# Sums of squares of the attention's heads: accumulated by ScalarE head by head, in place of one square and a reduction by VectorE

## The chip, the cores and the metric

The kernel runs on one core of one Trainium2 chip. The metric is the device time of one execution in microseconds (us), lower is better. The engines of a core are PE (TensorE, matmuls), DVE (VectorE), ACT (ScalarE), POOL (GpSimd) and SP (SyncE, here only a queue that issues transfers). Each takes its own instructions in the order in which the program lists them, and waits for the others by semaphores.

## The reference

Two layers of a trunk run over 640 tokens: 128 context tokens and 512 latent tokens that share the weights. In each layer the normed input goes through one projection `w_in`, and its columns feed three parallel mixers: a short gated convolution, windowed attention with 8 query heads and 2 key heads of 64, and a bidirectional gated DeltaNet. Their outputs go through `w_out`, and a SwiGLU channel mixer follows. What the change touches is the norm of queries and keys, per token and head:

```
def _rms(x, g):
    xf = x.astype(F32)
    y = xf * lax.rsqrt(jnp.mean(xf * xf, axis=-1, keepdims=True) + EPS)
    return (y * g.astype(F32)).astype(x.dtype)

q = _rms(q.reshape(bsz, n, N_Q_HEADS, HEAD_DIM), p['q_norm_g'])
k = _rms(k.reshape(bsz, n, N_KV_HEADS, HEAD_DIM), p['k_norm_g'])
```

For each token the squares of the 64 values of a head are summed: 8 sums for queries and 2 for keys.

## The kernel before, in words

Products are made in three passes of a high and a low part. A weight block of 128x1024 lands in `raw`, ACT rounds it to `whi` and DVE subtracts to get `wlo` (helper `split`, L172 and L173); PE multiplies high by high, high by low and low by high. L199, L201 and L202 are these three for products whose output has channels in its partitions (320 tokens at a time), and L627, L628 and L629 for products that have 128 tokens in their partitions.

The mixer of a layer is made of steps that a string of letters (`SEQ`) lists, among them `q` (queries of four heads, twice a layer), `k` (keys), `J` and `i` (inversion of triangular blocks for the DeltaNet), `h` and `g` (norm of DeltaNet queries `qd` and their products) and `s` (one step of the DeltaNet scan). The letters set the order in which the steps are written; the framework's scheduler then merges the instructions of neighbouring steps on each engine, by its own estimate of when each could run, so a step that gets other instructions can change the order of all those around it.

In the step `q`, PE makes for each of the 5 token tiles a product `pmm` of 128x256 (four heads), ACT copies it to `qv` (L1171), `headss` takes the squares (`asq`, L1077, ACT) and sums them per head into `qss` (L1078, DVE), and ACT's queue sends `qv` to memory (L1173). After the second `q` the inverse roots of all 40 sums are taken by DVE (`rsqrt_dve`, L219 to L234). The step `k` does the same with two heads a tile (`kraw`, `kss`). So `headss` runs 15 times in a layer: 10 times with four heads and 5 times with two.

What lies around the first `q`, in this order on DVE: the end of an inversion (L1010, L1012), its transposes (L1019 to L1022), the copies that PE's next products read (`adx`, L1029) and that make the inverse (`MK`, L1047), two `wlo` for the next weight blocks, then the sums of the DeltaNet queries (`dss`, L816, from the squares `dsq` that ACT makes at L814), their roots, the second inversion (L886 to L912) and the scaling of `qd` (L819). `scp` (L1148) is ACT's copy of a product of the short convolution, `scy` its convolution (L613 to L615), and `Ld` (L886) the blocks that the second inversion starts from.

Of the kernel before, what the change touches and what calls it, by code (L numbers as in the profile page):

```python
# [12 lines left out]
AF = mybir.ActivationFunctionType  # L13
ALU = mybir.AluOpType
AX = mybir.AxisListType
# [93 lines left out]
def hybrid_trunk_kernel(  # L109
# [8 lines left out]
    V, A, G, PE = nc.vector, nc.scalar, nc.gpsimd, nc.tensor  # L118
# [471 lines left out]
    def mixer(l, mp, hs, early_half, fill, first, later):  # L590
# [10 lines left out]
        def sm(tag, name, n, bufs):  # L601
            return mp.tile([128, n], F32, tag=tag, name=name, bufs=bufs)
# [471 lines left out]

        def headss(src, dst, nh):
            sq = sm("asq", "asq", 256, 2)
            A.activation(sq[:, 0:nh * 64], src, AF.Square)  # L1077
            V.tensor_reduce(out=dst, in_=sq[:, 0:nh * 64].rearrange("p (h d) -> p h d", d=64), axis=AX.X, op=ALU.add)  # L1078

        gcs = []  # L1080
        def tables():
# [83 lines left out]
        def queries(hb):  # L1165
            wq = [load_w(wslice(win, kk, 4, 768 + hb * 256, 256), 4, 256) for kk in (0, 4)]
            for t in range(NT):
                pt = pmm()
                tm_product(pt[:, 0:256], wq, t)
                qv = sm("qv", "qv", 256, 2)  # L1170
                A.copy(qv, pt[:, 0:256])  # L1171
                headss(qv, qss[:, t, hb * 4:hb * 4 + 4], 4)
                nc.scalar.dma_start(out=qscr[t, :, hb * 256:(hb + 1) * 256], in_=qv)  # L1173
            if hb == 1:
                rsqrt_dve(qss.rearrange("p t h -> p (t h)"), NT * 8, 1.0 / 64, EPS, ((rq.rearrange("p t h -> p (t h)"), lambda y: y, 0.125),), "q")


        def keys():
# [8 lines left out]
            for t in range(NT):  # L1187
                pt = pmm()
                tm_product(pt[:, 0:256], wkv, t)
                A.copy(kraw[:, t], pt[:, 0:128])  # L1190
                if t == 0:
                    nv = sm("qv", "nv", 256, 2)
                    A.copy(nv[:, 0:128], pt[:, 128:256])
                    nc.scalar.dma_start(out=new_v[0, l].rearrange("s v d -> s (v d)"), in_=nv[:, 0:128])
                put_values(pt[:, 128:256], t)
                headss(kraw[:, t], kss[:, t], 2)
# [355 lines left out]
    with tc.tile_pool(name="f0", bufs=1, reuse_waits="tile") as fp:  # L1552
# [14 lines left out]
        for t in range(NT):  # L1567
            sq = wp.tile([128, DM], F32, tag="raw", name="sqx", bufs=RAW_BUFS)
# [333 lines left out]
```

## Time and profile before

| | us |
|---|---|
| median of 3 runs | 1764.85 |
| lowest and highest of them | 1759.53, 1777.67 |
| the profiled execution, its own time | 1756.52 |
| its span, first to last instruction | 1754.6 |

Busy time of the profiled execution: PE 1663.1 us (95% of the span), DVE 1239.5 (71%), ACT 781.9 (45%), POOL 138.6 (8%). PE is the engine that is nearly always busy. A row of the timeline gives the start in us from the span's start, the duration, the engine, the line, the operation, the tiles and in brackets the time that the engine was idle before it and what it then waited for. Instructions of one engine that do not depend on each other overlap a little, so what an instruction takes from its queue is read from start to start.

### The profile page before, as it was taken

The numbers are of one execution on the slowest core, as the hardware profiler recorded it, in microseconds if no ns is written. First come the engines' busy times: TensorE is split into PE (matmuls) and PEld (weight loads), VectorE is DVE, ScalarE is ACT, GpSimd is POOL, SyncE is SP. The second block draws the span as 40 slices with busy tenths as digits, with TensorE's granted clock in tenths as the row PEclk, the third lists the DMA queues.
The fourth block names the chain that finished last, engine by engine and source line by source line (L and its number), as shares of the span: only waits on it lengthen the run. The fifth ranks groups of instructions, "written<-read, shape, count | busy, mean of one in ns | idle before, by whom it ended". The sixth has DMA issues, their size and how long they took to land. (4 is left out here: it accounts for less than half of the span.)

```text
span 1754.6 us, 34156 instructions
## 1 busy us (share of the span) xinstructions
PE 1663.1 (95%) x13677; PEld 1486.4 (85%) x13677; DVE 1239.5 (71%) x2780; ACT 781.9 (45%) x1620; POOL 138.6 (8%) x254
## 2 busy tenths in 40 slices
PE   6998999999999999999999889999998999999998
PEld 4887875488899999999988879655898999999998
DVE  4899667766856767667677994876578667667664
ACT  4555344645543433434465542555365343434342
POOL 1111112002000000000022001120030000000000
PEclk8998999999999999999999989999999999999999
DMA  9412233655534223222232221445722222222212
GB/s 341 130 49 71 87 98 130 210 162 162 156 117 127 85 70 88 77 87 66 73 116 61 64 72 58 151 151 160 239 72 83 87 74 73 85 84 76 81 61 61
DMA packets 207693, 188.42 MB, mean 107 GB/s; under 512 B 12782, under 2 KB 182702, under 8 KB 207534
## 3 DMA queue, kind: packets, MB, share of 16 engines
q1 hardware_dynamic: 192519, 170.97, 31.3%
q10 hardware_dynamic: 15015, 15.26, 2.7%
q8 instruction: 108, 1.77, 0.4%
q14 instruction: 51, 0.42, 0.1%
HBM read 168.64 MB, written 17.56 MB: 106 GB/s over the span
## 5 line engine op out<-in xcount | busy, mean ns | idle before, releaser
L172 ACT CAST whi<-raw 128x1024 fp32r<-128x1024 f32 (+1 forms) x102 | 100.0, 981 | 166.9 <-PE pmx L201 74.7
L173 DVE TENSOR_TENSOR wlo<-raw,whi 128x1024 fp32r<-128x1024 f32 (+1 forms) x102 | 115.8, 1138 | 24.5 <-ACT whi L172 24.2
L202 PE MATMUL pmm<-hh,wlo 128*128 128x320 f32 x336 | 108.0, 323 | 6.4 <-DVE wlo L173 6.3
L199 PE MATMUL pmm<-hh,whi 128*128 128x320 f32 x336 | 109.0, 326 | 4.5 <-ACT dnp L656 3.2
L582 DVE SCALAR_TENSOR_TENSOR xt<-pmx,mod,xt 128x128 f32<-128x128 f32 (+2 forms) x168 | 69.1, 434 | 50.4 <-PE pmx L202 48.5
L201 PE MATMUL pmm<-hl,whi 128*128 128x320 f32 x320 | 103.0, 322 | 0.0
L199 PE MATMUL pmm<-acth,whi 128*128 128x320 f32 x320 | 99.8, 312 | 1.7 <-DVE xt L582 1.7
L199 PE MATMUL pmx<-acth,whi 128*128 128x320 f32 x320 | 99.2, 310 | 0.1
L202 PE MATMUL pmm<-acth,wlo 128*128 128x320 f32 x320 | 99.2, 310 | 0.0
L201 PE MATMUL pmx<-actl,whi 128*128 128x320 f32 x320 | 99.0, 309 | 0.0
L201 PE MATMUL pmm<-actl,whi 128*128 128x320 f32 x320 | 98.9, 309 | 0.0
L202 PE MATMUL pmx<-acth,wlo 128*128 128x320 f32 x320 | 98.9, 309 | 0.0
L582 DVE SCALAR_TENSOR_TENSOR xt<-pmm,mod,xt 128x128 f32<-128x128 f32 (+2 forms) x168 | 68.6, 434 | 33.2 <-PE pmm L202 22.1
L172 ACT CAST whi<-rawd 128x1024 fp32r<-128x1024 f32 x40 | 42.0, 1050 | 102.8 <-PE pmx L201 93.9
L383 POOL TENSOR_TENSOR acc<-acc,sq 128x320 f32<-128x320 f32 x24 | 25.8, 1074 | 619.6 <-ACT sq L382 619.2
L202 PEld LDWEIGHTS pmm<-hh,wlo 128*128 128x128 f32 x336 | 65.3, 195 | 8.0 <-DVE wlo L173 7.2
L199 PEld LDWEIGHTS pmm<-hh,whi 128*128 128x128 f32 x336 | 65.6, 195 | 6.5 <-ACT dnp L656 4.0
L628 PE MATMUL pmm<-wlo,hh 128*128 128x256 f32 x240 | 69.8, 291 | 0.7 <-DVE wlo L173 0.6
L627 PE MATMUL pmm<-whi,hh 128*128 128x256 f32 x240 | 70.0, 293 | 0.0
L629 PE MATMUL pmm<-whi,hl 128*128 128x256 f32 x240 | 69.6, 290 | 0.0
L299 PE MATMUL pdn<-adaw,c 128*32 128x256 f32 x640 | 63.3, 399 | 5.4 <-DMA adaw<-in_ada_w_dram 5.4
L173 DVE TENSOR_TENSOR xlo<-rawo,xhi 128x1024 fp32r<-128x1024 f32 x40 | 49.0, 1224 | 27.2 <-ACT xhi L172 26.4
(560 smaller groups left out, 5587.2 us busy)
## 6 DMA issues: line engine op xcount, KB each, us to landing
adaw<-in_ada_w_dram SPq DMA_DIRECT2D x80, 512.0 KB, 4.1
raw<-in_w_down_dram SPq DMA_DIRECT2D x44, 512.0 KB, 3.4
raw<-in_w_in_dram SPq DMA_DIRECT2D x36, 512.0 KB, 3.8
rawo<-in_w_gate_dram SPq DMA_DIRECT2D x40, 256.0 KB, 3.6
rawd<-in_w_gate_dram SPq DMA_DIRECT2D x40, 256.0 KB, 3.4
rawd<-in_w_up_dram SPq DMA_DIRECT2D x40, 256.0 KB, 3.4
rawo<-in_w_up_dram SPq DMA_DIRECT2D x40, 256.0 KB, 3.2
araw<-in_ada_w_dram SPq DMA_DIRECT2D x16, 512.0 KB, 11.4
```

Source lines behind the costliest of these rows:

```text
L172: (hi_eng or A.copy)(hi, src)
L173: (lo_eng or V).tensor_tensor(out=lo, in0=src, in1=hi.bitcast(F32), op=ALU.subtract)
L199: mm(o, lhsT=wh[:, k], rhs=ah, start=k == 0, stop=False)
L201: mm(o, lhsT=wh[:, k], rhs=al, start=False, stop=False)
L202: mm(o, lhsT=wl[:, k], rhs=ah, start=False, stop=not lead and k == n - 1)
L299: mm(pr[32 * q:32 * q + 32, 0:256], lhsT=c32[:, k], rhs=raw[:, q * 256:(q + 1) * 256], start=k == 0, stop=k == 7)
L383: (G if k < 5 else V).tensor_tensor(out=self.acc[h], in0=self.acc[h], in1=sq, op=ALU.add)
L582: V.scalar_tensor_tensor(out=x[:, sl], in0=pt[:, a0:a1], scalar=gate[:, g:g + 1], in1=x[:, sl], op0=ALU.mult, op1=ALU.add)
L627: mm(pt, lhsT=ah[:, ts], rhs=wh[:, k % 4], start=k == 0, stop=False)
L628: mm(pt, lhsT=ah[:, ts], rhs=wl[:, k % 4], start=False, stop=False)
L629: mm(pt, lhsT=al[:, ts], rhs=wh[:, k % 4], start=False, stop=k == 7)
```

## The change

`headss` no longer squares a tile in one instruction and sums with DVE. It issues one ACT instruction for each head, which squares 64 columns and adds them up into the sum by itself (`accum_out`). On ACT 15 squares a layer become 50, each followed by the read of the accumulator; on DVE 15 reductions a layer go.

```
         def headss(src, dst, nh):
             sq = sm("asq", "asq", 256, 2)
-            A.activation(sq[:, 0:nh * 64], src, AF.Square)
-            V.tensor_reduce(out=dst, in_=sq[:, 0:nh * 64].rearrange("p (h d) -> p h d", d=64), axis=AX.X, op=ALU.add)
+            for h in range(nh):
+                A.activation(sq[:, h * 64:h * 64 + 64], src[:, h * 64:h * 64 + 64], AF.Square, accum_out=dst[:, h:h + 1])
```

The scheduler orders the steps around `q` and `k` anew. On ACT, around the end of the first `q` of layer 0, there stood before (`dsq` are the squares of the DeltaNet queries, `whi` two weight blocks):

```order
L1029 COPY adx<-DD 32x512
L814 ACTIVATE dsq<-qd 128x1024
L1171 COPY qv<-pmm 128x256
L1047 COPY MK<-TTq 32x16x32
L1077 ACTIVATE asq<-qv 128x256
L1173 DMA qscr<-qv 128x256
```

At the same place there now stands, from the second of the two `whi` on:

```order
L172 CAST whi<-raw 128x1024
L1173 DMA qscr<-qv 128x256
L1171 COPY qv<-pmm 128x256
L1047 COPY MK<-TTq 32x16x32
L1078 ACTIVATE asq,qss<-qv 128x64 x4
L1173 DMA qscr<-qv 128x256
L1047 COPY MK<-TTq 32x16x32
L1148 COPY scp<-pmm 128x128
L1148 COPY scp<-pmm 128x192
L1047 COPY MK<-TTq 32x16x32
L814 ACTIVATE dsq<-qd 128x1024
L814 ACTIVATE dsq<-qd 128x256
```

The squares `dsq` have moved from a place ahead of the two weight casts to one behind them, behind all squares of the queries and behind the copies of `scp`, which wait for a product of PE. In layer 1 they also stand behind the copies of `scp` now.

On DVE, at the same place of layer 0, there stood before (`adx` and `MK` belong to the first inversion, `dss` are the sums of `dsq`):

```order
L1029 COPY adx<-DD 32x512 x2
L1078 TENSOR_REDUCE qss<-asq 128x4
L1047 COPY MK<-TTq 32x16x32 x3
L173 TENSOR_TENSOR wlo<-raw,whi 128x1024
L1047 COPY MK<-TTq 32x16x32
L173 TENSOR_TENSOR wlo<-raw,whi 128x1024
L1078 TENSOR_REDUCE qss<-asq 128x4
L816 TENSOR_REDUCE dss<-dsq 128x16
```

And there now stands:

```order
L1029 COPY adx<-DD 32x512 x2
L1047 COPY MK<-TTq 32x16x32 x4
L173 TENSOR_TENSOR wlo<-raw,whi 128x1024 x2
L816 TENSOR_REDUCE dss<-dsq 128x16
L816 TENSOR_REDUCE dss<-dsq 128x4
```

The two reductions are gone, the last `MK` copy has moved ahead of the first `wlo`, and `dss` still follows directly behind the second `wlo`.

A little later on DVE, where the second inversion starts, the difference reads:

```order
 L891 STREAM_TRANSPOSE Ls<-Ld 64x1024
+L173 TENSOR_TENSOR wlo<-raw,whi 128x1024
+L614 SCALAR_TENSOR_TENSOR scy<-scp,vec_126,scy 128x642
 L231 SCALAR_TENSOR_TENSOR rsy<-rsw,rsy 128x16
 L892 STREAM_TRANSPOSE Ls<-Ld 64x32x32
+L615 SCALAR_TENSOR_TENSOR scy<-scp,vec_126,scy 128x642
 L227 TENSOR_TENSOR rsz<-rsx,rsy 128x16
```

A `wlo` and the two steps of the convolution, which stood some rows further down between those of the inversion, have moved ahead. On PE the transposes of `qd` (L824) have moved behind some 40 matmuls of the second `q`.

## Rows read from the trace of the kernel before

**Rows 1.** The page: its first line and part 1's line on PE

```profile
span 1754.6 us, 34156 instructions
PE 1663.1 (95%) x13677; PEld 1486.4 (85%) x13677; DVE 1239.5 (71%) x2780; ACT 781.9 (45%) x1620; POOL 138.6 (8%) x254
```

**Rows 2.** Windows: stretch, length, busy us (instructions) by engine, clock, DMA share, GB/s

```profile
132.00:152.00 20.00, 14.87 (x186) 14.33 (x185) 19.35 (x32) 13.10 (x25) 2.31 (x6) 0.91 0.21 67
152.00:176.00 24.00, 22.16 (x354) 20.55 (x353) 21.94 (x73) 9.56 (x20) 2.17 (x5) 0.86 0.27 76
994.00:1014.00 20.00, 15.86 (x175) 15.28 (x174) 19.26 (x33) 12.17 (x23) 1.75 (x5) 0.87 0.23 72
1014.00:1040.00 26.00, 23.68 (x397) 21.41 (x396) 23.81 (x79) 10.66 (x23) 2.79 (x5) 0.91 0.24 69
```

**Rows 3.** Timeline, PE: its waits for `wlo`, and matmuls behind two of them

```profile
150.94 0.63 PE L202 MATMUL pmm<-hh,wlo 128*128 128x320 f32 x1 [1.71 <-DVE wlo L173]
...
187.40 0.41 PE L202 MATMUL pmm<-hh,wlo 128*128 128x320 f32 x1 [2.06 <-DVE wlo L173]
...
189.12 0.31 PE L201 MATMUL pmm<-hl,whi 128*128 128x320 f32 x1
...
1049.67 0.64 PE L202 MATMUL pmm<-hh,wlo 128*128 128x320 f32 x1 [2.52 <-DVE wlo L173]
...
1053.20 0.31 PE L199 MATMUL pmm<-hh,whi 128*128 128x320 f32 x1
```

**Rows 4.** Lines L1077 and L1078: count, duration in ns (min/median/max), starts, shape

```profile
L1077 ACT ACTIVATE asq<-qv x20: 416/417/421, 132.8 to 1047.4; 128x256 f32<-128x256 f32 x20
L1077 ACT ACTIVATE asq<-kraw x10: 311/325/325, 217.9 to 1094.4; 128x128 f32<-128x128 f32 x10
...
L1078 DVE TENSOR_REDUCE qss<-asq x20: 367/414/423, 133.6 to 1050.7; 128x4 f32<-128x256 f32 x20
L1078 DVE TENSOR_REDUCE kss<-asq x10: 274/286/288, 218.3 to 1094.9; 128x2 f32<-128x128 f32 x10
```

**Rows 5.** Timeline, ACT: two squares with accumulation and the read between them

```profile
5.98 1.04 ACT L1569 ACTIVATE sqx<-xr 128x1024 f32<-128x1024 f32 x1
6.93 0.19 ACT L1569 ACTIVATION_READ_ACCUMULATOR sqx<-xr 128x1 f32 x1
7.02 1.04 ACT L1569 ACTIVATE sqx<-xr 128x1024 f32<-128x1024 f32 x1
```

**Rows 6.** Groups by shape, ACT: 64 columns from PSUM; busy us, mean ns

```profile
L682 ACT ACTIVATE vv<-pmx 128x64 f32<-128x64 f32 x8 | 1.4, 238 | 0.0
```

**Rows 7.** Timeline, DVE, layer 0, then two rows of layer 1

```profile
151.37 1.23 DVE L173 TENSOR_TENSOR wlo<-raw,whi 128x1024 fp32r<-128x1024 f32 x1
152.51 0.41 DVE L1078 TENSOR_REDUCE qss<-asq 128x4 f32<-128x256 f32 x1
152.84 1.54 DVE L816 TENSOR_REDUCE dss<-dsq 128x16 f32<-128x1024 f32 x2
...
170.19 0.76 DVE L857 TENSOR_TENSOR MQ<-pkq,MQ 128x256 f32<-128x256 f32 x2 [1.37 <-PE pkq L852]
...
186.13 2.35 DVE L173 TENSOR_TENSOR wlo<-raw,whi 128x1024 fp32r<-128x1024 f32 x2
...
1015.38 1.54 DVE L816 TENSOR_REDUCE dss<-dsq 128x16 f32<-128x1024 f32 x2
...
1048.39 2.36 DVE L173 TENSOR_TENSOR wlo<-raw,whi 128x1024 fp32r<-128x1024 f32 x2
```

**Rows 8.** Timeline, ACT: `dsq`, an `MK` copy and the `scp` copies

```profile
142.66 1.06 ACT L814 ACTIVATE dsq<-qd 128x1024 f32<-128x1024 f32 x1
...
149.52 0.61 ACT L1047 COPY MK<-TTq 32x512 f32<-32x512 f32 x1
...
156.44 0.49 ACT L1148 COPY scp<-pmm 128x128 f32<-128x128 f32 x2 [5.00 <-PE pmm L202]
...
1017.24 0.49 ACT L1148 COPY scp<-pmm 128x128 f32<-128x128 f32 x2 [4.98 <-PE pmm L202]
```

## The prediction

> **What bounds the kernel now.** I read the page first. PE is busy in 1663.1 of 1754.6 us [rows 1], so the kernel as a whole is bound by PE, and a change on another engine can only move the 91 us in which PE is not busy, and the time in which its clock is low. Next I cut the span into stretches and looked for those where PE is not full, and found two around the first queries of each layer, with the same picture: from 132 to 152 us PE is busy 14.87 of 20 us while DVE is busy 19.35, and from 994 to 1014 us PE 15.86 and DVE 19.26 [rows 2]. In the stretches behind them DVE is still at 21.94 of 24 and 23.81 of 26. There, and only there as far as this change goes, DVE sets the pace: the timeline of PE shows waits for DVE's `wlo` of 1.71, 2.06 and 2.52 us [rows 3]. ACT is busy 13.10 of 20 us in the first of these stretches [rows 2]: it has room, but not much more than the change will ask for. The keys (step `k`) lie outside, in a part where ACT and DVE wait for PE, so there I expect nothing.
>
> **What goes from DVE.** 30 reductions, 20 of 0.414 us and 10 of 0.286 us [rows 4], 11.1 us of busy time. In a solid queue one of the larger costs its start-to-start step, 152.51 to 152.84 = 0.33 us [rows 7]. In each layer ten of them lie in the stretch where DVE sets the pace. If nothing else moved, the `wlo` pair at 186.13 us [rows 7] would start nine steps, 3.0 us, sooner.
>
> **What comes to ACT.** 100 squares of 64 columns, each with a read of the accumulator. No row shows this shape, so I bound it. The squares of 128 and 256 columns take 0.325 and 0.417 us [rows 4]; on their line 64 columns take 0.28 us, and the one shape of 64 columns in the trace, from PSUM, takes 0.238 us [rows 6]. The read takes 0.19 us, but the next square starts 1.04 us after the one before, exactly its own duration [rows 5]: the read hides in the overlap of one instruction with the next. So a square with its read takes 0.24 to 0.28 us from the queue, or up to 0.28 + 0.19 = 0.47 us if for short squares nothing overlaps. I take 0.28, as the accumulating square of 1024 columns is the only row with the same pair. A tile of four heads then costs ACT 1.12 us in place of about 0.33 (0.417 less the overlap of 0.09), so 0.8 us more, and a tile of two heads 0.56 in place of 0.23. In all 20 x 0.8 + 10 x 0.33 = 19 us more on ACT; at 0.47 us a head it is 20 x 1.55 + 10 x 0.7 = 38 us.
>
> [...]
>
> Is the extra hidden? Five tiles fall into 132 to 152 us, 5 x 0.8 = 4.0 us on top of 13.10 [rows 2] makes 17.1 of 20 us, so ACT still has room, and the `whi` casts and the copies that free PE's banks come about when they came before. At 0.47 us it is 13.1 + 7.8 = 20.9 of 20 us, and the cover is gone.
>
> **What the new order costs.** This is the term on which the forecast rests. Before, ACT made `dsq` at 142.66 us [rows 8], ten us before DVE read it at 152.84 [rows 7]. Now `dsq` stands on ACT behind the `scp` copies and one `MK` copy. These copies wait for PE's first half tile of the short convolution: ACT sat idle 5.00 us before them, until 156.44 [rows 8]. DVE's side of this: with two reductions gone ahead of it (and two more further up) the first `wlo` lands about 0.5 us sooner, so PE's wait at 150.94 [rows 3] ends about 0.5 us sooner, and the `scp` copies start at about 155.95. They take 0.49 us, the `MK` copy 0.61, so `dsq` starts at about 157.0, takes 1.06 and ends at 158.05 [rows 8]. DVE has nothing else ahead of `dss` in its queue, having ended its second `wlo` at about 151.6 (151.37 + 1.23 less 1.0 [rows 7]), so it idles some 6 us and starts `dss` at 158.1 in place of 152.84: 5.2 us later. In layer 1 `dsq` now follows the copies of 1017.24 + 0.49 us [rows 8] and ends at 1018.8; `dss` starts there in place of 1015.38 [rows 7], 3.4 us later. (There the three `MK` copies have moved ahead of the `wlo`, which takes back what the removed reductions gave, so PE gains nothing at this wait.)
>
> Behind `dss` the same work remains in the queue up to the `wlo` pair at 186.13 and 1048.39 us; the `wlo` and the convolution that moved ahead only change places within it. What shortens it: four reductions, 4 x 0.33 = 1.3 us, and DVE's own wait of 1.37 us at 170.19 for PE [rows 7], of which I let 1.0 be taken up (bounds 0 and 1.37). So the pair comes 5.2 - 1.3 - 1.0 = 2.9 us later in layer 0 (2.5 to 3.9), and 3.4 - 1.3 - 1.0 = 1.1 us later in layer 1 (0.7 to 2.1). PE already waits for its first half at both places, 2.06 and 2.52 us [rows 3], so all of that is added to PE. Further waits of PE in between (it meets the transposes of `qd`, now later on both engines) only shift within this.
>
> **The clock.** After the wait of 2.52 us at 1049.67 the next 13 matmuls took 3.53 us, until 1053.20; after the wait of 2.06 us at 187.40, 11 took 1.72 us [rows 3], which for 13 would be 2.0. [...] A wait in layer 0 that grows to 5 us should look like the former: 1.5 us more (bounds 0, and 1.5 in each layer).
>
> **The sum** is 2.9 + 1.1 + 1.5 = 5.5 us, with bounds 3.2 and 9.0. The profiled execution took 1756.5 us and would become 1762.0. The three runs have a median of 1764.85, 8.3 us above the profiled one; all four together have 1762.2 in their middle, and on this I put the sum: 1767.5 us.
>
> **The rivals.**
>
> *DVE's relief comes through: faster.* If `dsq` were ready in time, DVE would keep its queue solid, the `wlo` pair would come 3.0 us sooner in each layer, and PE's waits of 2.06 and 2.52 us would vanish, with 0.5 us at 150.94 and the 1.5 us of low clock: 6.6 us, so 1755.6 us. It decides at one point: the delay at `dss` of 5.2 us must stay below the 2.3 us that the queue behind can take up, so `dsq` must end before about 155.1 us in layer 0. Against it is the order of ACT: the `scp` copies it now follows came at 156.44 us. [...] Chance 0.15.
>
> *It is all hidden: no change.* PE gets to both waits later for reasons of its own, or DVE's idle time in front of the pair is larger than I see, and the delay is taken up. For it speaks that DVE idles again soon after and that PE is busy 95%. Time 1762. Chance 0.2.
>
> *ACT becomes the bound: clearly slower.* If a head costs 0.47 us, ACT is asked for 20.9 of 20 us at 132 to 152 [rows 2], its copies of `qv` free PE's banks late, about 1 us in each layer, and a second low clock of 1.5 us follows each: 5 us on top of the forecast, 1772.5 us. It decides where a head costs more than 13.1 + 5 x (4u - 0.33) = 20 gives, u = 0.43 us. Against it is the hidden read [rows 5]. Chance 0.1.
>
> **How the numbers follow.** The forecast has 0.55, the rivals 0.15, 0.2 and 0.1. The predicted time is that of the likeliest. The range goes from the faster rival to the slow one with the spread of the runs (1759.5 to 1777.7) beside it: 1756 to 1779. The likeliest case alone has 1765 to 1771, by its bounds. A change of 1%, 17.6 us, is about what a measurement of this kernel can tell from none; all cases lie within it, and only their sum with an unseen shift of the order elsewhere leaves it. So faster by over 1% gets 0.03, within 1% gets 0.88, slower by over 1% gets 0.09.
>
> **What would show it.** In the changed profile: heads of 0.24 to 0.28 us with the next start no more than 0.3 us on; `dsq` directly behind the copies of `scp` at about 157 us; a hole of 5 to 6 us on DVE before `dss`, released by ACT; the wait of PE for the `wlo` pair longer than 2.06 us, about 5, with the clock at 1.2 GHz behind it, and in layer 1 about 3.5; nothing at the keys. The forecast is wrong if `dsq` ends before 155 us, if PE's waits there shrink, or if PE waits for ACT's copies of `qv`.

## The result, and the profile after

| | before | after |
|---|---|---|
| median of 21 runs, us | 1763.36 | 1774.22 |
| lowest and highest | 1758.58, 1777.67 | 1765.11, 1780.16 |
| span of the profiled execution | 1754.6 | 1771.8 |

The ratio after to before is 1.0052, with a 95% interval of 1.0039 to 1.0064: 9.2 us slower (6.9 to 11.3). The forecast was slower by 5.5 us and within 1%. It lay on the right side, and was too small: the 1774.2 us lie in its range of 1756 to 1779, but above the 1765 to 1771 of the likeliest case alone. (1762.2 and 5.5 make 1767.7 us; the prediction has 1767.5.)

The page of the changed kernel, its span and part 1's line on busy time (it answers [rows 1]):

```profile
span 1771.8 us, 34277 instructions
PE 1671.7 (94%) x13677; PEld 1494.1 (84%) x13677; DVE 1230.4 (69%) x2750; ACT 796.7 (45%) x1790; POOL 141.9 (8%) x254
```

DVE has 30 instructions fewer and 9.1 us less to do, ACT 14.8 us more, and PE, with the same instructions, is busy 8.6 us longer.

The timeline of ACT in the changed kernel, two heads of a tile and then what stands at `dsq` (it answers [rows 5, 8]):

```profile
140.58 0.24 ACT L1078 ACTIVATE asq<-qv 128x64 f32<-128x64 f32 x1
140.73 0.19 ACT L1078 ACTIVATION_READ_ACCUMULATOR asq<-qv 128x1 f32 x1
140.82 0.24 ACT L1078 ACTIVATE asq<-qv 128x64 f32<-128x64 f32 x1
...
155.56 0.49 ACT L1148 COPY scp<-pmm 128x128 f32<-128x128 f32 x2 [5.85 <-PE pmm L202]
156.07 0.62 ACT L1047 COPY MK<-TTq 32x512 f32<-32x512 f32 x1
156.72 1.37 ACT L814 ACTIVATE dsq<-qd 128x1024 f32<-128x1024 f32 x2
```

The timeline of DVE in the changed kernel, layer 0 and then four rows of layer 1 (it answers [rows 7]):

```profile
148.24 2.36 DVE L173 TENSOR_TENSOR wlo<-raw,whi 128x1024 fp32r<-128x1024 f32 x2
157.81 1.54 DVE L816 TENSOR_REDUCE dss<-dsq 128x16 f32<-128x1024 f32 x2 [7.21 <-ACT dsq L814]
...
173.95 0.76 DVE L857 TENSOR_TENSOR MQ<-pkq,MQ 128x256 f32<-128x256 f32 x2 [0.55 <-PE pkq L852]
...
176.80 0.76 DVE L857 TENSOR_TENSOR MQ<-pkq,MQ 128x256 f32<-128x256 f32 x2 [1.29 <-PE pkq L852]
...
179.40 0.76 DVE L857 TENSOR_TENSOR MQ<-pkq,MQ 128x256 f32<-128x256 f32 x2 [1.01 <-PE pkq L852]
...
190.38 2.36 DVE L173 TENSOR_TENSOR wlo<-raw,whi 128x1024 fp32r<-128x1024 f32 x2
...
1028.51 1.55 DVE L816 TENSOR_REDUCE dss<-dsq 128x16 f32<-128x1024 f32 x2 [5.23 <-ACT dsq L814]
...
1035.69 0.89 DVE L614 SCALAR_TENSOR_TENSOR scy<-scp,vec,scy 128x642 f32<-128x642 f32 x1 [1.52 <-ACT scy L613]
...
1046.57 0.76 DVE L857 TENSOR_TENSOR MQ<-pkq,MQ 128x256 f32<-128x256 f32 x2 [1.31 <-PE pkq L852]
...
1060.79 2.36 DVE L173 TENSOR_TENSOR wlo<-raw,whi 128x1024 fp32r<-128x1024 f32 x2
```

`dsq` stands behind the copies of `scp`, ACT sits idle 5.85 us ahead of them, and DVE has a hole of 7.21 us before `dss` in layer 0 and of 5.23 us in layer 1. In the solid rows of before there is no such hole [rows 7].

The timeline of PE in the changed kernel, its waits in the two layers (they answer [rows 3]):

```profile
170.91 1.09 PE L824 MATMUL pmx<-ident,qd 128*128 128x128 f32 x8 [2.37 <-DVE qd L819]
...
191.66 0.41 PE L202 MATMUL pmm<-hh,wlo 128*128 128x320 f32 x1 [2.90 <-DVE wlo L173]
...
1018.51 0.50 PE L199 MATMUL pmm<-hh,whi 128*128 128x320 f32 x1 [2.77 <-ACT whi L172]
...
1062.07 0.41 PE L202 MATMUL pmm<-hh,wlo 128*128 128x320 f32 x1 [2.52 <-DVE wlo L173]
```

**A ruler.** What lies ahead of these stretches shifts from one execution to the next: ACT's first copy of `qv` stands at 133.32 us (layer 0) and 1001.63 (layer 1) in one profile of a kernel and at 132.62 and 997.51 in another of the same (e5 and e11 below). So I measure the two stretches by themselves, from ACT's first copy of `qv` of a layer to the product of PE that has waited for the `wlo` pair (187.40 and 1049.67 in [rows 3]). These first copies are, in the kernel before:

```profile
132.44 0.37 ACT L1171 COPY qv<-pmm 128x256 f32<-128x256 f32 x1 [2.33 <-PE pmm L629]
...
994.83 0.37 ACT L1171 COPY qv<-pmm 128x256 f32<-128x256 f32 x1 [2.15 <-PE pmm L629]
```

and in the changed kernel:

```profile
132.16 0.37 ACT L1171 COPY qv<-pmm 128x256 f32<-128x256 f32 x1 [2.34 <-PE pmm L629]
...
1004.05 0.37 ACT L1171 COPY qv<-pmm 128x256 f32<-128x256 f32 x1 [2.15 <-PE pmm L629]
```

Layer 0 takes 187.40 - 132.44 = 54.96 us before and 191.66 - 132.16 = 59.50 after, 4.54 us more; layer 1 takes 54.84 and 58.02, 3.18 us more. Together that is 7.7 us. That lies within the measured interval. Behind the pair in layer 0 PE's clock falls as well (point 5 below).

### The profile page after: what moved, and what is told of

It reads as the page before. It is cut to its first block, busy times and chain, and to the rows that moved or that the text cites. A ratio compares the mean times of both kernels' runs of the same rounds, so it can differ in the third digit from the quotient of the medians.

```text
span 1771.8 us, 34277 instructions
## 1 busy us (share of the span) xinstructions
PE 1671.7 (94%) x13677; PEld 1494.1 (84%) x13677; DVE 1230.4 (69%) x2750; ACT 796.7 (45%) x1790; POOL 141.9 (8%) x254
```

## The experiments

Each row below was made in the same way from the rows of that kernel's trace. The last column is the measured ratio to the kernel before, turned into us.

| kernel | layer 0, us | layer 1, us | both | measured, us (95%) |
|---|---|---|---|---|
| changed | +4.5 | +3.2 | +7.7 | +9.2 (6.9 to 11.3) |
| e1 `dsq` ahead | +1.1 | +4.3 | +5.3 | +7.6 (3.3 to 11.8) |
| e2 `dsq` held, old arithmetic | +4.3 | +4.3 | +8.6 | +9.5 (5.3 to 13.7) |
| e3 queries only | +3.3 | +3.5 | +6.8 | +7.1 (3.0 to 11.3) |
| e4 keys only | -0.1 | -1.4 | -1.5 | +1.6 (-2.3 to 5.5) |
| e5 old order, new arithmetic | -1.1 | -2.5 | -3.6 | -3.0 (-6.2 to 0) |
| e11 e5 again | -1.1 | -2.6 | -3.7 | -2.3 (-6.5 to 1.8) |
| e6 new order, old arithmetic | +6.3 | +6.0 | +12.3 | +15.0 (10.2 to 19.7) |
| e7 old order on ACT alone | -2.4 | -0.9 | -3.3 | -2.8 (-5.8 to 0.2) |
| e8 sums left out, old order | -2.4 | -3.2 | -5.6 | -4.8 (-8.1 to -1.4) |
| e9 `MK` behind `whi` | +2.6 | +1.1 | +3.7 | +8.6 (4.9 to 12.1) |
| e10 as e7, `dsq` late | +4.8 | +5.0 | +9.8 | +14.6 (9.7 to 19.5) |
| e12 `MK` behind `whi`, `dsq` ahead | -1.4 | +1.2 | -0.2 | +3.7 (0.7 to 6.7) |

e5 and e11 are one and the same kernel, and their stretches agree within 0.1 us.

### One move at a time: e1 and e2

e1 adds one order to the changed kernel (`scp_cp` collects the copies of L1148):

```
-            A.activation(sq, src, AF.Square)
+            dq = A.activation(sq, src, AF.Square)
+            if not kind:
+                tc.add_manual_dep(scp_cp[0].ins, dq.ins.name, NOSYNC, reason="behind the squares")
...
```

> The changed kernel with one order added: ScalarE's squares of the DeltaNet queries (dsq, L814) must come ahead of the first copies of the convolution's half tile (scp, L1148), where the kernel before had them, in both layers; the head-by-head squares stay. Theory H (the late dsq makes the loss): VectorE's reduction dss starts near 153 us in layer 0 (157.8 in the changed kernel), its hole of 7.2 us shrinks under 2, and the 8 to 9 us go, so that the kernel comes to that of before or, with 10 reductions fewer per layer on VectorE, a little under: 1757 to 1765 us, where the kernel before has about 1763. Rival A (the longer squares on ScalarE hold back its other work, whi casts and qv copies, wherever dsq stands): dss moves, but the time stays within 3 us of the changed kernel, 1771 to 1776. Rival C (the clock of TensorE between the two layers' stages makes half of the loss): about 1768 to 1770.

Measured: +7.6 us. The loss did not go: the median was 1770.5 us, above the 1757 to 1765 of theory H. The timeline of DVE in e1, layer 0, then layer 1:

```profile
150.67 1.54 DVE L818 TENSOR_REDUCE dss<-dsq 128x16 f32<-128x1024 f32 x2
...
156.58 1.24 DVE L893 STREAM_TRANSPOSE Ls<-Ld 64x1024 f32<-64x1024 f32 x1 [2.48 <-ACT Ld L888]
159.62 1.23 DVE L173 TENSOR_TENSOR wlo<-raw,whi 128x1024 fp32r<-128x1024 f32 x1 [1.81 <-ACT whi L172]
...
1023.01 1.24 DVE L893 STREAM_TRANSPOSE Ls<-Ld 64x1024 f32<-64x1024 f32 x1 [2.46 <-ACT Ld L888]
...
1026.08 1.23 DVE L173 TENSOR_TENSOR wlo<-raw,whi 128x1024 fp32r<-128x1024 f32 x1 [1.82 <-ACT whi L172]
```

The timeline of PE in e1, at the `wlo` pair of layer 0:

```profile
187.42 0.42 PE L202 MATMUL pmm<-hh,wlo 128*128 128x320 f32 x1 [2.41 <-DVE wlo L173]
```

ACT takes `dsq` at 149.58 in e1, ahead of the copies of `scp` at 155.17, where in the changed kernel it took it at 156.72, behind them. `dss` starts at 150.67, the hole is gone, and DVE waits at the next places instead: 2.48 us for `Ld`, which ACT copies behind `scp`, 1.81 us for a `whi` behind that, and 1.51 us for ACT's `scy` at 162.35. In layer 0 the stretch is still 3.5 us shorter than in the changed kernel; in layer 1 nothing is won. There ACT's order has a second move, which the forecast had passed over. The timeline of ACT in the changed kernel, layer 1:

```profile
1016.07 0.62 ACT L1047 COPY MK<-TTq 32x512 f32<-32x512 f32 x1 [1.07 <-DVE TTq L1021]
...
1017.43 1.03 ACT L172 CAST whi<-raw 128x1024 fp32r<-128x1024 f32 x1
...
1018.62 1.03 ACT L172 CAST whi<-raw 128x1024 fp32r<-128x1024 f32 x1
```

and the same casts in the kernel before:

```profile
1006.61 1.98 ACT L172 CAST whi<-raw 128x1024 fp32r<-128x1024 f32 x2
```

From the layer's first `qv` copy the first cast came 11.78 us on before and comes 13.38 us on now: it stands behind a copy of `MK` that waits for DVE's transposes, and behind three heads; a fourth head separates the two casts. PE waits 2.77 us for it. e1 keeps this order.

e2 goes the other way: the kernel before, reductions and all, with `dsq` alone held.

```
-            A.activation(sq, src, AF.Square)
+            dq = A.activation(sq, src, AF.Square)
+            if not kind:
+                tc.add_manual_dep(dq.ins, scp_last[1].ins.name, NOSYNC, reason="held")
...
```

> The kernel before, with VectorE's reductions as they were, and only dsq (L814) held on ScalarE behind the two copies of the convolution's first half tile, in both layers. Theory H: the hold alone makes the loss; dss starts at 157 to 158 us, and since no reduction is taken out of VectorE's queue to shorten it, the loss is that of the changed kernel or a little more: +8 to +11 us, 1771 to 1774. By the sum on record without its shortening by the reductions: 5.2 + 3.4 + 1.5 = +10. Rival A (ScalarE's longer squares): within 1.5 us of the kernel before.

Measured: +9.5 us, with `dss` at 158.65 us behind an idle time of 5.15:

```profile
158.65 1.54 DVE L818 TENSOR_REDUCE dss<-dsq 128x16 f32<-128x1024 f32 x2 [5.15 <-ACT dsq L814]
```

So the hold, with what the scheduler moves around it, is enough for a loss of this size, but (e1) it is not the only thing that must be undone. The next experiments therefore tie the order itself.

### Queries and keys: e3 and e4

`headss` takes the new form for four heads only (e3), or for two only (e4, `nh == 2` in its place); the lines below are e3 against the kernel before:

```
+            if nh == 4:
+                for h in range(nh):
+                    A.activation(sq[:, h * 64:h * 64 + 64], src[:, h * 64:h * 64 + 64], AF.Square, accum_out=dst[:, h:h + 1])
+                return
             A.activation(sq[:, 0:nh * 64], src, AF.Square)
...
```

> Only the 20 query tiles (four heads each) are summed on ScalarE; the 10 key tiles keep one square and VectorE's reduction. ScalarE's order in the stretch of the inversions is that of the changed kernel, dsq late. Theory H, with the keys worth nothing: as the changed kernel, +8 to +10 us, 1771 to 1774. Rival K (the keys' part costs 2 us or more, by ScalarE's squares ahead of the copies for KTs or by VectorE): 1768 to 1771.

> Only the 10 key tiles (two heads each) are summed on ScalarE; the query tiles keep one square and VectorE's reduction, and dsq stands early on ScalarE as before. Theory H, with the keys worth nothing: the time of the kernel before within 1.5 us, 1761.5 to 1764.5. Rival K: 2 us or more above it, 1765 to 1768. With e3 it also tells whether the two parts add up to the whole.

Measured: +7.1 us for the queries and +1.6 (-2.3 to 5.5) for the keys. The loss belongs to the queries; that the keys are worth exactly nothing can't be told at this width.

### Order against arithmetic: e5 to e8, and e11

In these kernels every call to an engine is numbered as the kernel is written, and a list for each engine (`KEPT`) holds the order in which the other kernel has them; each call is tied behind the one ahead of it in the list. Their calls go through one wrapper, so all their rows carry its line, 129; they are read by the tiles' names.

```
...
+    for k_, s_ in KEPT.items():
+        seq = [REC[k_][a_ + i_] for r_ in s_.split() for a_, n_ in [map(int, (r_ + "+1").split("+")[:2])] for i_ in range(n_)]
+        for a_, b_ in zip(seq, seq[1:]):
+            tc.add_manual_dep(b_, a_.name, NOSYNC, reason="kept order")
```

> The changed arithmetic in the old order: squares head by head on ScalarE and no reductions on VectorE, but each instruction of TensorE, VectorE, ScalarE and GpSimd is tied to its place in the kernel before (the four or two squares of a tile stand where the one square stood). After e1 the theory is wider. Theory O (the loss is the order: not dsq alone, but also the whi casts that moved behind a copy of MK and between the head squares, and the scaling of qd on VectorE): no loss, 1757 to 1764 us, where the kernel before has about 1762.5; the dss reduction starts at 152.0 to 152.9, the wlo pair at 183 to 187. Theory A (ScalarE's longer squares cost the time in any order, by holding back whi and qv): 5 us or more above the kernel before, 1767 to 1772, with TensorE waiting for whi and qv at the places where it waits in the changed kernel.

> The old arithmetic in the new order: one square of a whole tile on ScalarE and VectorE's reductions as before, but each other instruction of the four engines is tied to its place in the changed kernel (the square of a tile stands where its last head stood). Theory O: the loss of the changed kernel, and the 20 to 30 reductions back on VectorE on top, +8 to +13 us, 1771 to 1776. Theory A: within 2 us of the kernel before.

> As e5, but only ScalarE's instructions are tied to the order of the kernel before; TensorE, VectorE and GpSimd are ordered anew around it. Theory O, with the order on ScalarE as the cause: as e5, 1757 to 1765 us. If VectorE's own order (what stands behind dss) carries a part of the loss: 1766 to 1770. Theory A: as e5, 1767 to 1772.

> e5 once more, to see whether the new arithmetic in the old order is faster than the kernel before: by e5 3 us less, 1757 to 1761 against some 1762.5; by the other reading of e5's interval, no difference.

The four answer the question: the new arithmetic in the old order loses nothing (e5 -3.0, e11 -2.3, e7 -2.8 us), the old arithmetic in the new order loses 15.0, more than the 8 to 13 expected. Theory A, that ScalarE's longer squares cost the time, has fallen, and tying ScalarE's order alone (e7) is as good as tying all four engines. The timeline of DVE in e5, layer 0:

```profile
153.02 1.54 DVE L129 TENSOR_REDUCE dss<-dsq 128x16 f32<-128x1024 f32 x2
...
185.95 2.36 DVE L129 TENSOR_TENSOR wlo<-raw,whi 128x1024 fp32r<-128x1024 f32 x2
```

and in e6:

```profile
161.02 1.54 DVE L129 TENSOR_REDUCE dss<-dsq 128x16 f32<-128x1024 f32 x2 [6.57 <-ACT dsq L129]
```

The first has no idle time ahead of `dss`, the second has the hole of the changed kernel with the old squares. e5 and e11 are the version that comes out under both kernels: together, each weighted by the inverse square of its interval's width, they lie 2.7 us under the kernel before (0.3 to 5.2), but neither interval by itself leaves zero out.

> What the relief of VectorE is worth at most: the kernel before in its own order with the 30 reductions left out and nothing put in their place (the sums of squares are set to a constant once per layer, so the sums are not computed; ScalarE's squares stay). By the rival that the relief comes through, worked out on record: 6.6 us less, about 1756, with the wlo pair near 183.1 us in layer 0. If VectorE waits for others behind the removed reductions all the same (as in e1, where dss came 2.2 us sooner and the wlo pair did not): 0 to 3 us less, 1760 to 1763.

Measured: -4.8 us (-8.1 to -1.4). This kernel leaves the sums out, so it shows only what their time is worth. The relief of DVE is real, and it reaches the end of the kernel when no order moves. The traces give 5.6 us for the reductions gone (e8) and 3.6 with the heads' squares added on ACT (e5), so by the traces the squares take back some 2 us; the measured times, -4.8 and -3.0, agree, but their intervals overlap.

### How few moves: e9, e10 and e12

e10 is e7 with only `dsq` put back behind `scp` in ScalarE's list (and two copies of `Ld`, whose buffer comes from the pool of `dsq`, behind it).

> As e7 (squares head by head, ScalarE in the order of the kernel before), but with dsq alone moved back behind the first two copies of scp, and the two copies of Ld that stood ahead of them behind dsq. What dsq's place costs by itself under the new arithmetic: theory H (the step on record) 5 to 8 us above e7, 1765 to 1769; if the place of dsq matters only together with the late whi, within 2 us of e7, 1759 to 1762. From the start of the queries to the wlo pair: +4 to +5 us in layer 0 and +2 to +4 in layer 1 against e7.

Measured: +14.6 us, and 13.1 us more than e7 in the two stretches (7.1 and 5.9). Theory H had 5 to 8 us above e7; by the last column of the table the two are 17 us apart. DVE's holes in e10, in its timeline of layer 0 and layer 1:

```profile
157.97 1.55 DVE L129 TENSOR_REDUCE dss<-dsq 128x16 f32<-128x1024 f32 x2 [6.45 <-ACT dsq L129]
...
1025.87 1.55 DVE L129 TENSOR_REDUCE dss<-dsq 128x16 f32<-128x1024 f32 x2 [5.72 <-ACT dsq L129]
```

6.45 + 5.72 = 12.2 us, nearly the whole difference to e7 in the stretches: on balance nothing behind the hole takes it up. But the hole is not alone. In both layers DVE waits another 1.5 us behind it for `scy` (at 165.18 and 1033.03), which it does not in e7, and the orders of DVE and PE, which are not tied here, have changed as well.

e9 holds only the four `MK` copies of ScalarE behind the second `whi` (in layer 0 of the kernel before, two of the four stood ahead of it); e12 adds e1's order.

```
...
+            for cp in mk_cp if hb else ():
+                tc.add_manual_dep(cp.ins, casts[-2].ins.name, NOSYNC, reason="behind the cast")
```

> The changed kernel with one tie: ScalarE's four copies of MK behind the first inversion (L1047) must come behind the cast whi of the second half of the query weights, as in the kernel before. With the copies held, the ordering puts dsq (1024 columns) into the room this makes, ahead of the whi pair, as before; the squares of the last 256 columns stay behind the copies of scp. Theory O with few moves carrying the loss (dsq, and whi behind a copy of MK): most of the loss goes, 1758 to 1764 us. If the rest of the moves matters as well (copies of qd and kqT, Ld): 1766 to 1771, as e1.

> e9 and e1 together: the copies of MK behind the cast whi, and both squares dsq (1024 and 256 columns) ahead of the copies of scp. If few moves carry the loss: 1757 to 1763 us, at or under e9. If VectorE then only waits at the next place, as in e1 (for Ld and whi): 1764 to 1768.

Measured: +8.6 and +3.7 us. In e9 the 1024 columns of `dsq` came early by themselves, but the last 256 stayed behind `scp`, and DVE's timeline in e9 shows it waiting for these:

```profile
157.88 0.42 DVE L817 TENSOR_REDUCE dss<-dsq 128x4 f32<-128x256 f32 x1 [2.14 <-ACT dsq L815]
```

With both parts early (e12) layer 0 gains 1.4 us and layer 1 still loses 1.2; DVE waits there 1.52 us for `scy`, at 1028.99 (point 4 below). By the measured times a few ties get more than half of the loss back, not all of it. Of e9's 8.6 us the two stretches show only 3.7; where the rest comes from is open.

## Why the prediction was right, and where its sizes were off

1. **What goes from DVE**: right. 30 reductions went, and in the old order this shows as 4.8 us (e8); the rival that the relief comes through had it at 6.6.

2. **The price of a head**: the heads came at 0.24 us from start to start (140.58 to 140.82), the lower end of the 0.24 to 0.28 that I read from the rows, not the 0.28 that I took, and ACT's busy time grew by 14.8 us, not 19. The bound of 0.47 us was far off, and with it the rival that ACT becomes the bound. "Hidden" was nearly right: what was not hidden is the place of the casts in layer 1, which is order, and the some 2 us between e8 and e5 in the traces.

3. **The hole**: right in place and size. `dsq` at 156.72 (forecast 157.0), `dss` at 157.81 (158.1), a hole of 7.21 us (some 6). By the ruler `dss` is 5.25 us later in layer 0 (25.65 us after the first copy, 20.40 before; forecast 5.2) and 3.91 in layer 1 (24.46 and 20.55; forecast 3.4). e2 and e10, where `dsq` was put behind `scp`, have this hole and the loss again. As other work moved around it in both, they show what the late `dsq` costs with all that follows from it, not the hole by itself.

4. **What the queue behind takes up**: the term that was mis-sized. Forecast 1.3 us by the reductions and 1.0 of DVE's own wait for PE, 2.3 in each layer. Measured: from `dss` to the `wlo` pair 33.29 us before and 32.57 after in layer 0, 33.01 and 32.28 in layer 1, so 0.7 us in each. The windows between these two rows, with the columns of [rows 2], in the kernel before:

```profile
152.84:186.13 33.29, 30.66 (x463) 28.39 (x461) 30.90 (x88) 13.92 (x28) 2.37 (x6) 0.91 0.21 62
...
1015.38:1048.39 33.01, 29.45 (x474) 26.70 (x473) 30.77 (x88) 14.86 (x31) 3.39 (x7) 0.95 0.18 52
```

and in the changed kernel:

```profile
157.81:190.38 32.57, 27.34 (x457) 24.02 (x455) 29.05 (x84) 17.99 (x65) 2.42 (x6) 0.90 0.14 42
...
1028.51:1060.79 32.28, 26.33 (x465) 23.56 (x463) 28.67 (x83) 17.82 (x65) 4.90 (x6) 0.95 0.14 42
```

   The third busy time is DVE's. It fell by 1.85 and 2.10 us, more than I had taken; but DVE's idle time, which I let shrink by 1.0, grew: 33.29 - 30.90 = 2.39 became 3.52, and 2.24 became 3.61. I had treated the wait for PE's products of `qd` as slack. In layer 0 it is a wait for an engine that the same delay holds up: PE waited 2.37 us for `qd` at 170.91 and ran slowly behind it. The window of these products in the changed kernel:

```profile
173.30:180.00 6.70, 6.70 (x65) 5.86 (x65) 3.78 (x15) 0.66 (x4) 0.00 (x0) 0.57 0.00 1
```

   and the window of the same products in the kernel before:

```profile
169.00:176.00 7.00, 7.00 (x102) 6.06 (x102) 5.37 (x20) 2.01 (x6) 0.00 (x0) 1.00 0.09 32
```

   65 matmuls in 6.7 us at a granted clock of 0.57, against 102 in 7.0 us at 1.00. In the kernel before the clock was low too behind PE's wait for `qd`, at 0.50, but for a shorter time and ahead of these products, on matmuls of the queries:

```profile
165.70:169.00 3.30, 3.30 (x17) 3.15 (x15) 3.12 (x16) 1.02 (x2) 0.00 (x0) 0.50 0.26 75
```

   That the clock is what made DVE wait there is read from these rows and was not tried by itself.

   In layer 1 the wait for these products did not grow: 1.31 us at 1046.57, where the kernel before had 1.29 at 1033.11. The added idle time there is the wait of 1.52 us for ACT's `scy` at 1035.69. The prediction had the convolution, which the new order moved ahead on DVE, "only change places" in the queue; but its input was late, because POOL's step on `scp` took longer (ACT waited 2.05 us for it, 0.38 in the kernel before). In the timeline of POOL, layer 1, it reads in the kernel before:

```profile
1022.06 0.75 POOL L1149 TENSOR_TENSOR scp<-scp,csb 128x320 f32<-128x320 f32 x1 [2.38 <-ACT scp L1148]
```

   and in the changed kernel:

```profile
1032.37 2.42 POOL L1149 TENSOR_TENSOR scp<-scp,csb 128x320 f32<-128x320 f32 x1 [1.93 <-ACT scp L1148]
```

   In the profiles of the kernel before and of the changed kernel this step of 320 columns took 0.75 to 0.78 us the three times that no `wlo` of DVE ran beside it, 1.47 us the four times that one ran beside it for about 0.86 us, and 2.42 us here, beside the whole `wlo` at 1033.00 (1.17 us). That the one engine holds up the other is read from these times and was not tried. The wait of 1.5 us for `scy` stands in layer 1 of the changed kernel, e3, e6, e9 and e12, in both layers of e2 and e10 and in layer 0 of e1 (0.87 us in its layer 1), and in none of e5, e7, e8 and e11.

   So the pair came 4.53 us later in layer 0 (forecast 2.9) and 3.18 in layer 1 (1.1).

5. **The clock behind the pair**: right in layer 0. The window behind it in the changed kernel:

```profile
192.60:196.00 3.40, 3.40 (x14) 2.72 (x12) 2.38 (x11) 0.00 (x0) 0.00 (x0) 0.51 0.91 281
```

   and behind the shorter wait of the kernel before:

```profile
187.40:191.00 3.60, 3.60 (x32) 3.15 (x33) 3.50 (x11) 0.30 (x1) 0.00 (x0) 1.00 0.68 193
```

   The traces give the clock as a share of full speed, and no run shows the 1.2 GHz that the forecast names: the share was 0.51 in these 3.4 us, and behind the wait of 2.52 us in the kernel before it was 0.52 from 1049.67 to 1053.20. As an estimate, 3.4 us at 0.51 are 1.7 us lost, forecast 1.5. Not all of it lasts. ACT's last copy of the keys' product, `kraw`, some 43 us behind the pair in each layer, stands in the kernel before at

```profile
230.32 0.27 ACT L1190 COPY kraw<-pmm 128x128 f32<-128x128 f32 x1 [0.39 <-PE pmm L629]
...
1094.10 0.27 ACT L1190 COPY kraw<-pmm 128x128 f32<-128x128 f32 x1 [0.39 <-PE pmm L629]
```

   and in the changed kernel at

```profile
235.72 0.27 ACT L1190 COPY kraw<-pmm 128x128 f32<-128x128 f32 x1 [0.39 <-PE pmm L629]
...
1106.15 0.27 ACT L1190 COPY kraw<-pmm 128x128 f32<-128x128 f32 x1 [0.39 <-PE pmm L629]
```

   From the layer's first copy of `qv` that is 97.88 and 99.27 us before, 103.56 and 102.10 after: 5.7 and 2.8 us more. So behind the pair layer 0 lost another 1.1 us, and layer 1 got some 0.3 back. Together that is 8.5 us, where 9.2 (6.9 to 11.3) was measured.

6. **How it would show**: half wrong. I expected PE's wait for the pair at about 5 us, and 3.5 in layer 1; it was 2.90 and 2.52. PE came to it late itself, from waits for `whi` and `qd` and from the low clock ahead. That the pair's delay reaches PE was right; PE's wait at that place was the wrong thing to look for.

7. **The rivals**: "the relief comes through if `dsq` ends before 155.1" has the wrong condition. In e1 it ended before 151, and the kernel was slower by 7.6 us all the same. What decides is the whole order on ScalarE (e7), `dsq`, the `whi` pair and the `Ld` copies among it.

## What to carry to other kernels

Work taken off a busy engine is worth what the trace says only if the order of everything around it stays; where a scheduler orders anew, compare the two orders on every engine, and look for each instruction that now stands behind one that waits. To tell order from arithmetic, tie the old order and run the new arithmetic in it: here that turned 9.2 us of loss into a gain of 2.7 (0.3 to 5.2). When a delay is pushed through a queue, don't let a wait for another engine take it up before asking whether that engine is held up by the same delay.

## What the runs showed that I had not expected

The same stretch, from the pair of layer 0 to the first copy of layer 1, in which of the change little more than the five key tiles of layer 0 lies, took between 804.0 (e8) and 816.8 us (e3) in the profiles, 807.4 before and 812.4 after. Single executions can't be compared there; by the ruler ten of the thirteen kernels in the table came out within 3.1 us of the measured difference, while e9, e10 and e12 were measured 4 to 5 us slower than it says. Carried on to the last copy of `kraw`, the ruler gives 12.2 us for e10, within 2.4 of the measurement, so part of that loss falls behind the pair; e9 (5.0) and e12 (-0.3) stay 3.6 and 4.0 us short, which is not explained. And the late `dsq` cost more in the otherwise old order (e10, 9.8 us in the stretches) than in the order that the scheduler made around it (7.7). The measured times, 14.6 and 9.2 us, have intervals that overlap, so this is not settled.
